# One trunk layer on one core: small products of the recurrence queued with the filler, three squares left unadded, the last gate pair in two halves of tokens

## The chip, the cores and the metric

The kernel runs on one core of one Trainium2 chip. The time is device microseconds of one execution; three executions of the kernel before gave 2769.55, 2764.9 and 2765.1 us, median 2765.1. A core has TensorE (PE; PEld is its loading of weights), VectorE (DVE), ScalarE (ACT), GpSimd (POOL) and SyncE (SP), which starts the transfers.

## The reference

1024 tokens, 2048 channels, one layer. An RMS norm over the channels of each token comes first; one combined projection makes the inputs of two branches. One is a recurrence over 16 heads of 64 (RWKV-7), the other attends to a selection of keys. Both are gated, joined and projected; then comes a second gate, which multiplies a projection of p, and a last RMS norm.

```python
def rms_norm(x, g, eps=NORM_EPS):
    xf = x.astype(jnp.float32)
    y = xf * lax.rsqrt(jnp.mean(xf * xf, axis=-1, keepdims=True) + eps)
...
# per head and step of the recurrence
        Sa = jnp.einsum('bhvk,bhk->bhv', S, a_t)
        S = (S * w_t[:, :, None, :] + Sa[..., None] * b_t[:, :, None, :]
             + v_t[..., None] * k_t[:, :, None, :])
        y = jnp.einsum('bhvk,bhk->bhv', S, r_t)
...
    bonus = jnp.sum(rh * kh * r_k.astype(f32), axis=-1, keepdims=True) * vh
...
# after both branches: h += W_out(concat); h += (p W_ple) * sigmoid(h W_pg); RMS norm
```

## The kernel before

Channels lie on the 128 partitions and tokens on the free axis, in two halves (hf) of TH = 512. A float32 projection product is made of three products of rounded parts (fp32r): wh·xh, wh·xl, wl·xh; wh is a copy by ScalarE, wl = w - wh a subtraction by GpSimd, in two pieces of 256 columns each. Small products in plain float32 take two passes of TensorE and stand in the trace as two matmuls.

No engine's order is written by hand. All operations are recorded, and a planner (`plan`, line 267) with costs and due times places each on its engine; each carries a level, and the lower one goes first. For TensorE it keeps three queues (line 304): ops under level LG = 3 are the work that is due; ops at LG and above are the filler, RUN = 3 of which may follow one another after a burst; ops with LEND = 0.5 wait for the end of a burst, or until they are WAIT = 3 us old, or until nothing else is there (lines 308 to 315). The transposes pk and pv (lines 720 and 729) and those of chunk_out (815) are LEND already.

Stages. (1) From 0 to some 1480 us: `load_xn` (484) loads 16 tiles of x for a half, splits them, and squares each (level LSQ) into xsum, by an add on VectorE; buffers zs (NZ = 3) hold the squares. `x_row` (470) takes the token sums by `token_sums` (477), a product of each 128 tokens of xsum with a column of ones; then a reciprocal root on GpSimd (rpow) and a spreading over the partitions by `bcast` (463), four transposes into a PSUM tile named cr. `zgroup` (550) is the combined projection. The recurrence goes over 8 units of two heads and their four quarters of 256 tokens, 32 sub-units, each of NCK = 4 chunks: `chunk_setup` (616) makes pA, pb2 (702) and, in `side_a` (709), pa, four products whose masked result is AA; `chunk_serial` (762) runs the chain pu, UV, pS, and ends each chunk with a product of AA and UV added to pY. These use the PSUM ring pi (3 buffers). (2) The key search and the attention, to some 2000 us; it starts with the products pg of hq and the scores pix of qs. (3) The end: `wout_ds` (1426) adds the output product for a half, with dh and dl from `split_mixed` (1380); `gate` (1448) makes, for each of 16 tiles, pl (6 products, tile pg), pz (48 products), tanh, the sum h2 and its square sq, which GpSimd adds to acc; `pss` are the token sums of acc and of the last square; `emit_out` (1475) makes rr and rb_, a copy of cr by ScalarE, scales each tile by it, eleven on VectorE and every third on ScalarE and GpSimd, and stores each tile (256 KB). Order as recorded: output product and gate of half 0, output product of half 1, output of half 0, gate of half 1, output of half 1. Rings at the end: 5 temporary tiles (tmp3), 5 raw weight tiles, 6 each of wh and wl, 2 buffers of pi. The level LEVAC = 1 of what leaves PSUM, and of emit_out(0), lies ahead of LG, at which the splits dh and dl and the products of the gate are recorded.

Of the kernel before, what the change touches and what calls it, by code (L numbers as in the profile page):

```python
# [20 lines left out]
D = 2048  # L21
# [364 lines left out]
def hybrid_kernel(ctx, tc, cst, msk, bkt, prm, xt, pt_, w_z, w_z80, w_lora, w_uq, w_iq, w_uk, w_uv, w_o, w_pg,  # L386
# [61 lines left out]
    sm = pool(ph1r, RP, name="sm", bufs=4, side="right")  # L448

    W_, PI = [NWR, NWH], [3]  # L450
    XH, XL, SB = [None] * 4, [None] * 4, [None] * 2

    def nhalf(dst):
        if len(dst.shape) == 2:
# [14 lines left out]

    def x_row(hf):  # L470
        sr = sm.tile([128, 4], F32, name="sr", bufs=1)
        nc.vector.tensor_scalar(sr, token_sums(SB[hf], 128), 1.0 / D, 1e-6, op0=OP.mult, op1=OP.add)
        rpow(sr, sr)
        SB[hf] = wp.tile([128, TH], F32, name="SB", tag="SB", bufs=1)
        nc.scalar.activation(SB[hf], bcast(sr), AF.Copy)

    def token_sums(t, n):

        pn = ps.tile([128, 4], F32, name="cn", tag="pi", bufs=PI[0])
        for i in range(4):  # L480
            nc.tensor.matmul(pn[:, i:i + 1], t[:n, i * 128:i * 128 + 128], one[:n], start=True, stop=True)
        return pn

    def load_xn(hf, g, piece=None):
        XH[g] = xn.tile([128, 4, TH], F32R, name=f"xh{g}", tag=f"xh{g}")
        XL[g] = xn.tile([128, 4, TH], F32R, name=f"xl{g}", tag=f"xl{g}")
        for k in range(4):
            if hf == 0:
                r = io.tile([128, TH], F32, name=("r", "k", "v", "gg")[k])
            else:  # L490
                r = wp.tile([128, TH], F32, name="xr", tag="wr", bufs=NWR)
            nc.sync.dma_start(r, xt[(g * 4 + k) * 128:(g * 4 + k + 1) * 128, hf * TH:hf * TH + TH])
            gc = col(P, PNG + g * 4 + k)
            nc.scalar.activation(XH[g][:, k, :], r, AF.Copy, scale=gc)
            nc.vector.scalar_tensor_tensor(XL[g][:, k, :], r, gc, XH[g][:, k, :], op0=OP.mult, op1=OP.subtract)
            with nc.level(LSQ):
                if g == k == 0:
                    SB[hf] = tp.tile([128, TH], F32, name="xsum", tag="zl", bufs=3)
                    nc.scalar.activation(SB[hf], r, AF.Square)
                else:  # L500
                    sq = tp.tile([128, TH], F32, name="zsq", tag="zs", bufs=NZ)
                    nc.scalar.activation(sq, r, AF.Square)
                    nc.vector.tensor_tensor(SB[hf], SB[hf], sq, op=OP.add)
            if piece and k in PIECES:
                piece()
# [110 lines left out]
    def chunk_setup(s_, u, t0, wa, lw_, tiles):  # L616
# [83 lines left out]
        for h in range(2):  # L700
            nc.scalar.activation(AB[hp(h), :, hp(h)], AR[hp(h), :, hp(h)], AF.Copy)
        pb2 = ps.tile([128, TQ], F32, name="pb2", tag="pi", bufs=3)
        nc.tensor.matmul(pb2, rkb, rk, start=True, stop=True)
        bonv = io.tile([128, TQ], F32, name="bonv", bufs=2)
        nc.vector.tensor_tensor(bonv, pb2, v, op=OP.mult)
        sl = lambda t: (lambda h, c: t[hp(h), c, :])
# [1 line left out]

        def side_a():
            pa = ps.tile([128, NCK, 128], F32, name="pa", tag="pi", bufs=3)  # L710
            for c in range(NCK):
                nc.tensor.matmul(pa[:, c, :], KB[:, c, :], BR[:, c, :], start=True, stop=True)
            nc.vector.tensor_tensor(AA, pa.rearrange("p c (h t) -> p c h t", h=2), c_("incl")[:, None, None, :].to_broadcast(
                [128, NCK, 2, 64]), op=OP.mult)

# [46 lines left out]
    def chunk_serial(u, last, after, AA, AB, Q, KBT, UV, BR, Wx, bonv):  # L762

        pY = ps.tile([128, NCK, 128], F32, name="pY", tag="py", bufs=1)
        if not after[1]:
            for h in HO:
                nc.scalar.activation(UV[hp(h), 0, hp(h)], S[u][hp(h)], AF.Copy)
        for c in range(NCK):  # L770
            pch = ps.tile([128, 3, 128], F32, name="pch", tag="pu", bufs=1)
            pr_, pu, pS = pch[:, 0], pch[:, 1], pch[:, 2]
            nc.tensor.matmul(pr_, AB[:, c, :], UV[:, c, :], start=True, stop=True)
            rh = sm.tile([128, 128], F32, name="rh", bufs=2)
            nc.vector.tensor_copy(rh, pr_)
            nc.tensor.matmul(pY[:, c, :], BR[:, c, :], UV[:, c, :], start=(c == 0), stop=False, skip_group_check=True)
            more = not (last and c == NCK - 1)
            if more:
                Sw = sm.tile([128, 64], F32, name="Sw", bufs=2)
                for h in HO:  # L780
                    nc.scalar.activation(Sw[hp(h)], UV[hp(h), c, hp(h)], AF.Copy, scale=Wx[hp(h), c, 64:65])
            nc.tensor.matmul(pu, Q[:, c, :], rh, start=True, stop=True)
            for h in HO:
                nc.scalar.activation(UV[hp(h), c, hp(h)], pu[hp(h), hp(h)], AF.Copy)
            if more:
                nc.tensor.matmul(pS, KBT[:, c, :], UV[:, c, :], start=True, stop=True)
                for h in HO:
                    if c < NCK - 1:
                        to = UV[hp(h), c + 1, hp(h)]
                    elif after[0] is not None:  # L790
                        to = after[0][hp(h), 0, hp(h)]
                    else:
                        to = S[u][hp(h)]
                    nc.vector.scalar_tensor_tensor(to, pS[hp(h), hp(h)], Wx[hp(h), c, 64:65], Sw[hp(h)],
                                                   op0=OP.mult, op1=OP.add)
            nc.tensor.matmul(pY[:, c, :], AA[:, c].rearrange("p h t -> p (h t)"), UV[:, c, :], start=False, stop=True,
                             skip_group_check=True)
        return pY

    def chunk_out(u, hf, q, y, bonv, gg):  # L800
# [23 lines left out]
    def sum_rows(zs, n):  # L824

        acc = None
        for z in zs:
# [2 lines left out]
            if acc is not None:  # L830
                nc.gpsimd.tensor_tensor(sq[:n], acc[:n], sq[:n], op=OP.add)
            acc = sq
        return token_sums(acc, n)

    def chan_rms(pn, width):
        a = sm.tile([128, 4], F32, name="ca", bufs=2)
# [224 lines left out]
    def pg_tile():  # L1061
        return g_pool[0].tile([128, 512], F32, name="pg", tag=g_pool[1])
# [382 lines left out]
            nc.vector.tensor_tensor(PL[:, k, :], r, PH[:, k, :], op=OP.subtract)  # L1445
        return PH, PL

    def gate(hf, HH, HL, PH, PL):
        H2 = []
        acc = tp.tile([128, TH], F32, name="acc", bufs=1)  # L1450
        for n in range(16):
            pl = pg_tile()
            gemm_part(pl, w_pl[n, 0], 128, 0, 2, 2, lambda k: PH[:, k, :], lambda k: PL[:, k, :])
            pz = gemm(lambda g: w_pg[n, g], 128, 16, lambda k: HH[k], lambda k: HL[k])
            with nc.level(LEVAC):
                tg = tmp3("tg3")
                nc.scalar.activation(tg, pz, AF.Tanh, scale=0.5)
                nc.vector.scalar_tensor_tensor(tg, tg, 1.0, pl, op0=OP.add, op1=OP.mult)
                h2 = mp.tile([128, TH], F32, name=f"h2{n}", tag=f"h2{n}")
                nc.vector.tensor_tensor(h2, HH[n], HL[n], op=OP.add)  # L1460
                nc.vector.scalar_tensor_tensor(h2, tg, 0.5, h2, op0=OP.mult, op1=OP.add)
                sq = acc if n == 0 else tmp3("sq3")
                nc.scalar.activation(sq, h2, AF.Square)
                if 0 < n < 15:
                    nc.gpsimd.tensor_tensor(acc, acc, sq, op=OP.add)
            H2.append(h2)
        pss = ps.tile([128, 4], F32, name="pss", tag="pss", bufs=1)
        with nc.level(LEVAC):
            for a in (acc, sq):
                for i in range(4):  # L1470
                    nc.tensor.matmul(pss[:, i:i + 1], a[:, i * 128:i * 128 + 128], one, start=(a is acc and i == 0),
                                     stop=(a is sq), skip_group_check=True)
        return H2, pss

    def emit_out(hf, H2, pss):
        ra = sm.tile([128, 4], F32, name="ra")
        nc.vector.tensor_scalar(ra, pss, 1.0 / D, 1e-6, op0=OP.mult, op1=OP.add)
        rr = sm.tile([128, 4], F32, name="rr")
        rpow(rr, ra)
        rb_ = tmp3("rb")  # L1480
        nc.scalar.activation(rb_, bcast(rr), AF.Copy)
        for n in range(16):
            if n % 3 == 2:
                nc.scalar.activation(H2[n], H2[n], AF.Copy, scale=col(P, PFG + n))
                nc.gpsimd.tensor_tensor(H2[n], H2[n], rb_, op=OP.mult)
            else:
                nc.vector.scalar_tensor_tensor(H2[n], H2[n], col(P, PFG + n), rb_, op0=OP.mult, op1=OP.mult)
            store(out[n * 128:n * 128 + 128, hf * TH:hf * TH + TH], H2[n])

    with nc.level(LG):  # L1490
        H0 = wout_ds(0)
        P0 = load_p(0)
        G0 = gate(0, *H0, *P0)
        P1 = load_p(1)
        H1 = wout_ds(1)
        with nc.level(LEVAC):
            emit_out(0, *G0)
        emit_out(1, *gate(1, *H1, *P1))
    nc.emit()
    ph3.close()  # L1500
    w2s.close()
# [39 lines left out]
```

## Time and profile before

| | |
|---|---|
| three executions, median | 2765.1 us (2764.9 to 2769.55) |
| the profiled execution | 2767.54 us |
| its span (first to last instruction) | 2765.7 us |
| mean granted clock of TensorE | 0.989 of full speed |
| TensorE busy | 2679.8 us, 97% of the span |
| VectorE, ScalarE, GpSimd busy | 1555.7, 1483.1, 1191.6 us |
| moved by DMA | 391.23 MB, 141 GB/s in the mean |

The profiled execution is one of the same program. Times of the trace count from the start of the span. In a row, `x8` is the number of instructions, and the time of a merged row runs from the start of the first to the end of the last; `out<-in` are the kernel's tile names; a wait is the idle time of the engine ahead of the instruction, with what released it. A matmul's duration includes its passing through the array, so one that follows another starts before the other's end.

### The profile page before, as it was taken

The page shows a single profiled execution, that of the slowest core. Times are in us where ns is not written, and L with a number is a line of the kernel's source. Part 1 is how long each engine was busy: PE and PEld are TensorE (multiplying, and loading weights), DVE is VectorE, ACT ScalarE, POOL GpSimd, SP SyncE. Part 2 cuts the span into 40 slices and gives each one's busy share as a digit, 9 for nine tenths or more (in the row PEclk, how much of TensorE's full clock was granted, in tenths as well). Part 3 has the DMA queues.
Part 4 walks back from the last instruction along what each step waited for, and adds up shares of the span by engine and source line. Part 5 has one row for each costly group of instructions (what it writes and reads, how often), then busy time and mean ns, then how long its engine had stood idle before and what let it go on. Part 6 is the DMA issues. An engine that isn't in the chain of part 4 may idle for free. (4 is left out here: it accounts for less than half of the span.)

```text
span 2765.7 us, 47714 instructions
## 1 busy us (share of the span) xinstructions
PE 2679.8 (97%) x16482; PEld 2150.6 (78%) x16482; DVE 1555.7 (56%) x3709; ACT 1483.1 (54%) x3265; POOL 1191.6 (43%) x1587
## 2 busy tenths in 40 slices
PE   7999999999999999999999999998999999999996
PEld 6777788877778777877787788786777778878885
DVE  5456676636674366666663678868767531135212
ACT  5445555535664355555554667786777533333331
POOL 7555556555411122222220543024433556657764
PEclk9999999999999999999999999999999999999998
DMA  7554444354454533334346557841222433355332
GB/s 235 156 183 124 134 141 142 119 170 136 138 191 157 168 120 122 124 124 125 124 132 192 161 202 241 269 153 52 75 81 85 153 105 98 96 165 176 99 97 93
DMA packets 229810, 391.23 MB, mean 141 GB/s; under 512 B 33552, under 2 KB 55104, under 8 KB 229568
## 3 DMA queue, kind: packets, MB, share of 16 engines
q1 hardware_dynamic: 229568, 388.18, 44.8%
q8 instruction: 130, 2.13, 0.3%
q14 instruction: 112, 0.92, 0.1%
HBM read 281.76 MB, written 101.08 MB: 138 GB/s over the span
## 5 line engine op out<-in xcount | busy, mean ns | idle before, releaser
L382 POOL TENSOR_TENSOR wl<-wr,wh 128x256 fp32r<-128x256 f32 (+1 forms) x840 | 664.6, 813 | 480.6 <-ACT wh L382 449.2
L382 ACT ACTIVATE wh<-wr 128x512 fp32r<-128x512 f32 (+1 forms) x624 | 383.5, 617 | 664.9 <-PE pz L382 534.5
L382 PE MATMUL pz<-xh,wh 128*128 128x512 f32 (+1 forms) x1504 | 611.1, 408 | 11.1 <-ACT wh L382 8.5
L382 PE MATMUL pz<-xl,wh 128*128 128x512 f32 (+1 forms) x1504 | 612.9, 409 | 0.0
L382 PE MATMUL pz<-xh,wl 128*128 128x512 f32 (+1 forms) x1504 | 607.8, 406 | 1.1 <-POOL wl L382 0.9
L382 PEld LDWEIGHTS pz<-xh,wh 128*128 128x128 f32 (+1 forms) x1504 | 286.0, 190 | 62.9 <-ACT wh L382 11.3
L382 PEld LDWEIGHTS pz<-xh,wl 128*128 128x128 f32 (+1 forms) x1504 | 285.2, 190 | 48.5 <-POOL wl L382 2.6
L382 PEld LDWEIGHTS pz<-xl,wh 128*128 128x128 f32 (+1 forms) x1504 | 285.7, 190 | 45.0
L382 PE MATMUL pz<-hl,wh 128*128 128x512 f32 x512 | 199.4, 390 | 0.1
L382 PE MATMUL pz<-hh,wh 128*128 128x512 f32 x512 | 199.3, 389 | 0.2 <-ACT wh L382 0.2
L382 PE MATMUL pz<-hh,wl 128*128 128x512 f32 x512 | 199.3, 389 | 0.0
L382 DVE SCALAR_TENSOR_TENSOR tg<-tg,pg 128x512 f32<-128x512 f32 x32 | 22.0, 687 | 308.7 <-ACT tg L382 297.4
L382 DVE CAST_PREDICATED QX<-MS,pq 128x512 f16<-128x512 uint8 x160 | 110.2, 689 | 134.6 <-PE pq L382 133.7
L382 ACT ACTIVATE Ztb<-pzt 64x256 f16<-64x256 f32 x320 | 120.5, 377 | 50.3 <-PE pzt L382 44.4
L382 POOL TENSOR_TENSOR mb<-mk,bt 128x256 f32<-128x256 f32 (+1 forms) x128 | 90.5, 711 | 117.8 <-DVE mx L382 101.6
L382 ACT ACTIVATE lgt<-lgt,nm 128x256 f32<-128x256 f32 (+7 forms) x128 | 98.7, 774 | 30.1 <-DVE nm L382 28.1
L382 PEld LDWEIGHTS pz<-hl,wh 128*128 128x128 f32 x512 | 96.1, 188 | 20.6 <-DVE hl L382 0.5
L382 PEld LDWEIGHTS pz<-hh,wh 128*128 128x128 f32 x512 | 96.1, 188 | 20.4 <-ACT wh L382 0.6
L382 PEld LDWEIGHTS pz<-hh,wl 128*128 128x128 f32 x512 | 96.1, 188 | 19.9
L382 ACT ACTIVATE scratch<-mk,th 128x1024 f16<-128x1024 f32 (+2 forms) x93 | 96.8, 1041 | 21.8 <-DVE xm L382 13.1
L382 ACT ACTIVATE PT<-ptt 128x512 f32<-128x512 f32 (+1 forms) x160 | 83.8, 551 | 43.1 <-PE ptt L382 41.7
L382 ACT ACTIVATE Sw<-UV,Wx 64x64 f32<-64x64 f32 x240 | 82.4, 343 | 44.5 <-DVE UV L382 40.3
(331 smaller groups left out, 5893.6 us busy)
## 6 DMA issues: line engine op xcount, KB each, us to landing
wr<-in_w_z_dram SPq DMA_DIRECT2D x368, 256.0 KB, 2.9
low<-wl SPq DMA_DIRECT2D x184, 256.0 KB, 3.2
wl<-low SPq DMA_DIRECT2D x184, 256.0 KB, 2.6
wr<-in_w_pg_dram SPq DMA_DIRECT2D x128, 256.0 KB, 2.6
wr<-in_w_o_dram SPq DMA_DIRECT2D x88, 256.0 KB, 2.9
h<-h SPq DMA_DIRECT2D x60, 256.0 KB, 3.5
h<-in_xt_dram SPq DMA_DIRECT2D x32, 256.0 KB, 3.4
out_dram<-h SPq DMA_DIRECT2D x32, 256.0 KB, 2.3
```

The costliest lines, as they stand in the source:

```text
L382: getattr(self.real[o.eng], o.name)(*o.args, **o.kw)
```

## The change

1. `pb2`, the four products pa of `side_a`, and the product of AA and UV that ends each chunk's pY are recorded at LEND.
2. In `load_xn`, the squares of the last three tiles (g == 3, k = 1 to 3) stay in their zs buffers; `token_sums` takes a list and adds the four operands in PSUM, 16 products instead of 4, in both halves of tokens.
3. `gate` of half 1 runs tiles 14 and 15 as two halves of 256 tokens each: both tiles for the first 256, then both for the second, with weights loaded, copied and split for each. Their squares are not added to acc. `emit_out` is called for each half of 256, with three operands of the token sums, and it now contains the pss products; VectorE scales from the PSUM tile pb (cr) itself, GpSimd's tiles still from the copy rb_. The h2 tiles become four group tiles of four, and a group is stored by one transfer: 1 MB for half 0, 512 KB for each half of half 1. For half 0, sums are acc and the square of tile 15 as before.

```diff
     def x_row(hf):
-        nc.vector.tensor_scalar(sr, token_sums(SB[hf], 128), 1.0 / D, 1e-6, op0=OP.mult, op1=OP.add)
+        nc.vector.tensor_scalar(sr, token_sums([SB[hf], *SQ[hf]], 128), 1.0 / D, 1e-6, op0=OP.mult, op1=OP.add)
...
-            nc.tensor.matmul(pn[:, i:i + 1], t[:n, i * 128:i * 128 + 128], one[:n], start=True, stop=True)
+            for t in ts:
+                nc.tensor.matmul(pn[:, i:i + 1], t[:n, i * 128:i * 128 + 128], one[:n], start=(t is ts[0]), stop=(t is ts[-1]))
...
             with nc.level(LSQ):
-                if g == k == 0:
+                if g == 3 and k > 0:
+                    sq = tp.tile([128, TH], F32, name="zsq", tag="zs", bufs=NZ)
+                    nc.scalar.activation(sq, r, AF.Square)
+                    SQ[hf].append(sq)
+                elif g == k == 0:
...
-        nc.tensor.matmul(pb2, rkb, rk, start=True, stop=True)
+        with nc.level(LEND):
+            nc.tensor.matmul(pb2, rkb, rk, start=True, stop=True)
...
-            for c in range(NCK):
-                nc.tensor.matmul(pa[:, c, :], KB[:, c, :], BR[:, c, :], start=True, stop=True)
+            with nc.level(LEND):
+                for c in range(NCK):
+                    nc.tensor.matmul(pa[:, c, :], KB[:, c, :], BR[:, c, :], start=True, stop=True)
...
-            nc.tensor.matmul(pY[:, c, :], AA[:, c].rearrange("p h t -> p (h t)"), UV[:, c, :], start=False, stop=True,
-                             skip_group_check=True)
+            with nc.level(LEND):
+                nc.tensor.matmul(pY[:, c, :], AA[:, c].rearrange("p h t -> p (h t)"), UV[:, c, :], start=False, stop=True,
+                                 skip_group_check=True)
...
+    def gate(hf, HH, HL, PH, PL, split=()):
+        H2[hf] = [mp.tile([128, 4, TH], F32, name=f"h2{hf}{g}", tag=f"h2{g}") for g in range(4)]
+        runs = [([n for n in range(16) if n not in split], (0, TH))]
+        runs += [(split, (t, t + TQ)) for t in range(0, TH, TQ)] if split else []
+        for ns, (t0, t1) in runs:
...
+                    if 0 < n < (14 if split else 15):
+                        nc.gpsimd.tensor_tensor(acc, acc, sq, op=OP.add)
+                    else:
+                        sqs.append(sq)
+            if ns is split:
+                with nc.level(LEVAC):
+                    emit_out(hf, [acc[:, t_], *sqs], t0, t1)
...
+    def emit_out(hf, sums, t0, t1):
+        pss = ps.tile([128, nb], F32, name="pss", tag="pss", bufs=1)
+        for j, a in enumerate(sums):
+            for i in range(nb):
+                nc.tensor.matmul(pss[:, i:i + 1], a[:, i * 128:i * 128 + 128], one, start=(i == j == 0),
+                                 stop=(j == len(sums) - 1), skip_group_check=True)
...
+                if n % 3 == 2:
+                    nc.scalar.activation(h2, h2, AF.Copy, scale=col(P, PFG + n))
+                    nc.gpsimd.tensor_tensor(h2, h2, rb_, op=OP.mult)
+                else:
+                    nc.vector.scalar_tensor_tensor(h2, h2, col(P, PFG + n), pb, op0=OP.mult, op1=OP.mult)
+            store(out[g * 512:g * 512 + 512, hf * TH + t0:hf * TH + t1].rearrange("(n p) t -> p n t", p=128),
+                  H2[hf][g][:, :, t0:t1])
...
-        emit_out(1, *gate(1, *H1, *P1))
+        gate(1, *H1, *P1, split=(14, 15))
```

## Rows read from the trace of the kernel before

**Rows 1.** The page's first part: busy us (share of the span), instructions, by engine.
```profile
PE 2679.8 (97%) x16482; PEld 2150.6 (78%) x16482; DVE 1555.7 (56%) x3709; ACT 1483.1 (54%) x3265; POOL 1191.6 (43%) x1587
```

**Rows 2.** Busy time by engine, 100 to 1480 us; then granted clock, DMA share, GB/s.
```profile
100.00:1480.00 1380.00, 1366.17 (x9531) 1086.93 (x9530) 825.43 (x1747) 744.11 (x1905) 509.60 (x723) 1.00 0.45 141
```

**Rows 3.** The chain that ended last, its end: start us, us, what.
```profile
2717.27 10.88 PE pz L382 x48
...
2728.15 1.36 PE pg L382 x6
...
2741.43 0.61 ACT tg L382
...
2746.16 0.17 DVE ra L382
...
2746.40 1.03 POOL rr L382
...
2747.47 1.13 PE cr L382 x4
```

**Rows 4.** Timeline of the end: start us, us, what [idle before, releaser].
```profile
2749.31 12.50 DVE L382 SCALAR_TENSOR_TENSOR h<-h,P,rb 128x512 f32<-128x512 f32 x11 [2.99 <-ACT rb L382]
2749.35 7.93 POOL L382 TENSOR_TENSOR h<-h,rb 128x512 f32<-128x512 f32 x5 [1.94 <-ACT rb L382]
2751.19 11.14 SPq L382 DMA_DIRECT2D out_dram<-h  x16
```

**Rows 5.** Timeline of a weight piece in the last gate tile: ScalarE, GpSimd.
```profile
2725.38 0.63 ACT L382 ACTIVATE wh<-wr 128x512 fp32r<-128x512 f32 x1 [2.09 <-PE pz L382]
...
2726.09 1.44 POOL L382 TENSOR_TENSOR wl<-wr,wh 128x256 fp32r<-128x256 f32 x2 [1.28 <-ACT wh L382]
```

**Rows 6.** Groups by form: busy us, mean ns of one, idle before and releasers.
```profile
L382 DVE SCALAR_TENSOR_TENSOR kkn<-k,P,pb 128x256 f32<-128x256 f32 x32 | 15.3, 478 | 11.5 <-PE pb L382 11.3
...
L382 DVE SCALAR_TENSOR_TENSOR zl<-zl,P,cr 128x512 f32<-128x512 f32 x10 | 7.0, 744 | 4.3 <-PE cr L382 4.2
...
L382 ACT ACTIVATE sq<-y 128x256 f32<-128x256 f32 x32 | 13.2, 413 | 8.0 <-DVE y L382 7.5
```

**Rows 7.** Timeline, TensorE, products of 256 columns in a row.
```profile
1844.90 0.40 PE L382 MATMUL pg<-lv,CH 128*128 128x256 f32 x2
1845.14 0.40 PE L382 MATMUL pg<-hv,CL 128*128 128x256 f32 x2
```

**Rows 8.** Timeline of the start, first half's token sums.
```profile
46.41 0.63 ACT L382 ACTIVATE zsq<-gg 128x512 f32<-128x512 f32 x1 [0.43 <-DVE xsum L382]
46.89 2.95 DVE L382 TENSOR_TENSOR xsum<-xsum,zsq 128x512 f32<-128x512 f32 x3 [0.52 <-DVE xsum L382]
...
49.90 1.87 PE L382 MATMUL cn<-one,xsum 128*128 128x1 f32 x8 [6.24 <-DVE xsum L382]
```

**Rows 9.** Timeline, TensorE, second half's token sums.
```profile
807.25 0.95 PE L382 MATMUL cn<-one,xsum 128*128 128x1 f32 x8
```

**Rows 10.** Timeline, TensorE, one sub-unit of the recurrence.
```profile
1195.13 0.59 PE L382 MATMUL pb<-rk,rkb 128*128 128x256 f32 x2
1195.56 1.05 PE L382 MATMUL pA<-ARb,KB 128*128 128x128 f32 x8
1196.45 1.06 PE L382 MATMUL pa<-BRb,KB 128*128 128x128 f32 x8
```

**Rows 11.** Timeline, from the first gate half to the second half's output product.
```profile
2454.90 1.05 PE L382 MATMUL pss<-one,sq 128*128 128x1 f32 x8 [1.88 <-ACT sq L382]
...
2464.18 1.96 DVE L382 TENSOR_TENSOR dl<-mraw,dh 128x512 fp32r<-128x512 f32 x2 [3.87 <-ACT dh L382]
...
2525.99 0.58 ACT L382 ACTIVATE rb<-cr 128x512 f32<-128x512 f32 x1
```

**Rows 12.** Waits of TensorE, 1480 to 1700 us: us in total, times, longest.
```profile
PE pix L382 <- DVE qs L382: 6.1, 1, 6.1
PE pg L382 <- ACT hq L382: 3.6, 1, 3.6
```

More of the change, by code (lines that the diff above doesn't have):

```diff
@@ L450, in hybrid_kernel @@
     W_, PI = [NWR, NWH], [3]
-    XH, XL, SB = [None] * 4, [None] * 4, [None] * 2
+    XH, XL, SB, SQ = [None] * 4, [None] * 4, [None] * 2, [[], []]
     def nhalf(dst):
@@ L475, in x_row, with token_sums @@
         nc.scalar.activation(SB[hf], bcast(sr), AF.Copy)
-    def token_sums(t, n):
+    def token_sums(ts, n):
         pn = ps.tile([128, 4], F32, name="cn", tag="pi", bufs=PI[0])
         for i in range(4):
-            nc.tensor.matmul(pn[:, i:i + 1], t[:n, i * 128:i * 128 + 128], one[:n], start=True, stop=True)
+            for t in ts:
+                nc.tensor.matmul(pn[:, i:i + 1], t[:n, i * 128:i * 128 + 128], one[:n], start=(t is ts[0]), stop=(t is ts[-1]))
         return pn
@@ L832, in sum_rows @@
             acc = sq
-        return token_sums(acc, n)
+        return token_sums([acc], n)
     def chan_rms(pn, width):
@@ L1446, in load_p @@
         return PH, PL
-    def gate(hf, HH, HL, PH, PL):
-        H2 = []
+    H2 = [None] * 2
+    def gate(hf, HH, HL, PH, PL, split=()):
+        H2[hf] = [mp.tile([128, 4, TH], F32, name=f"h2{hf}{g}", tag=f"h2{g}") for g in range(4)]
         acc = tp.tile([128, TH], F32, name="acc", bufs=1)
[L1451 to L1473, printed above, removed]
@@ L1475, in emit_out @@
-    def emit_out(hf, H2, pss):
-        ra = sm.tile([128, 4], F32, name="ra")
+        runs = [([n for n in range(16) if n not in split], (0, TH))]
+        runs += [(split, (t, t + TQ)) for t in range(0, TH, TQ)] if split else []
+        for ns, (t0, t1) in runs:
+            t_ = slice(t0, t1)
+            sqs = []
+            for n in ns:
+                pl = pg_tile()[:, :t1 - t0]
+                gemm_part(pl, w_pl[n, 0], 128, 0, 2, 2, lambda k: PH[:, k, t_], lambda k: PL[:, k, t_])
+                pz = pz_tile()[:, :t1 - t0]
+                for g in range(4):
+                    gemm_part(pz, w_pg[n, g], 128, 4 * g, 4, 16, lambda k: HH[k][:, t_], lambda k: HL[k][:, t_])
+                with nc.level(LEVAC):
+                    tg = tmp3("tg3")[:, :t1 - t0]
+                    nc.scalar.activation(tg, pz, AF.Tanh, scale=0.5)
+                    nc.vector.scalar_tensor_tensor(tg, tg, 1.0, pl, op0=OP.add, op1=OP.mult)
+                    h2 = H2[hf][n // 4][:, n % 4, t_]
+                    nc.vector.tensor_tensor(h2, HH[n][:, t_], HL[n][:, t_], op=OP.add)
+                    nc.vector.scalar_tensor_tensor(h2, tg, 0.5, h2, op0=OP.mult, op1=OP.add)
+                    sq = (acc if n == 0 else tmp3("sq3"))[:, :t1 - t0]
+                    nc.scalar.activation(sq, h2, AF.Square)
+                    if 0 < n < (14 if split else 15):
[3 more added lines that the diff above has]
+            if ns is split:
+                with nc.level(LEVAC):
+                    emit_out(hf, [acc[:, t_], *sqs], t0, t1)
@@ L1477, in emit_out @@
+        return acc, sqs[-1]
+    def emit_out(hf, sums, t0, t1):
+        nb = (t1 - t0) // 128
+        pss = ps.tile([128, nb], F32, name="pss", tag="pss", bufs=1)
[3 more added lines that the diff above has]
+                                 stop=(j == len(sums) - 1), skip_group_check=True)
+        ra = sm.tile([128, nb], F32, name="ra")
         nc.vector.tensor_scalar(ra, pss, 1.0 / D, 1e-6, op0=OP.mult, op1=OP.add)
-        rr = sm.tile([128, 4], F32, name="rr")
+        rr = sm.tile([128, nb], F32, name="rr")
@@ L1479, in emit_out @@
         rpow(rr, ra)
[L1480 to L1488, printed above, removed]
+        pb = ps.tile([128, TH], F32, name="cr", tag="pi", bufs=PI[0])[:, :t1 - t0]
@@ new lines, in emit_out @@
+        for i in range(nb):
+            nc.tensor.transpose(pb[:, i * 128:i * 128 + 128], rr[:, i:i + 1].to_broadcast([128, 128]), ident)
+        rb_ = tmp3("rb")[:, :t1 - t0]
+        nc.scalar.activation(rb_, pb, AF.Copy)
+        for g in range(4):
+            for n in range(4 * g, 4 * g + 4):
+                h2 = H2[hf][g][:, n % 4, t0:t1]
+                if n % 3 == 2:
[5 more added lines that the diff above has]
+                  H2[hf][g][:, :, t0:t1])
@@ L1492, in hybrid_kernel @@
         P0 = load_p(0)
-        G0 = gate(0, *H0, *P0)
+        sums = gate(0, *H0, *P0)
         P1 = load_p(1)
@@ L1496, in hybrid_kernel @@
         with nc.level(LEVAC):
-            emit_out(0, *G0)
-        emit_out(1, *gate(1, *H1, *P1))
+            emit_out(0, sums, 0, TH)
+        gate(1, *H1, *P1, split=(14, 15))
     nc.emit()
```

## The prediction

> **What bounds the kernel now.** I read the page's busy shares first: TensorE is busy 97% of the span, every other engine at most 56% [rows 1]. So only three things count: TensorE's own work, its few idle stretches, and what lies behind its last product. The recurrence is no idle stretch: from 100 to 1480 us TensorE is busy 1366.17 of 1380.00 us at full granted clock [rows 2]; its chain of small products is filled up with projection products. The chain of waits ends with the gate: one gate tile is 1.36 us of pg and 10.88 us of pz products, 12.24 us, and behind the last of them tanh (from 2741.43), squares, sums, reciprocal root and its spreading over the partitions follow one by one [rows 3]. The timeline of that end shows eleven scalings on VectorE, 12.50 us from 2749.31, beside five on GpSimd and 16 stores [rows 4]. The span ends at 2765.7, so 24.3 us stand behind the last product. The profiled execution took 2767.54 us, 1.84 more than its span and 2.4 more than the median of the runs; I sum differences and take them off the median.
>
> **Change 1: pb2, pa and the second pY product at the filling queue's place.** Nothing is added; 9 products in each of 32 sub-units change place. A pair of 256-column ones takes at most 0.59 us, eight of pa at most 1.06 us [rows 10], wherever they stand. TensorE runs without a gap there, so a product moved costs the same later: nothing, while filler is at hand. What it can bring is latency: pb2 and pa no longer stand ahead of the chain's next product (pb2, then pA, then pa is the order now [rows 10]), so the recurrence could end earlier; then filler must be found for the time after it. The waits to be filled stand at the start of the second stage: 3.6 us for hq and 6.1 us for qs [rows 12]. Against it: each of these ops now waits up to 3 us for a burst's end, and behind pa wait VectorE's mask (AA), behind that pY and the output of the unit; a buffer of the three in the ring pi is held as long. Bounds: -7, both waits (9.7) but for about a quarter that I leave to hq's and qs's own steps, and +5, the share of a gap where filler runs out (a third of the 13.8 us idle in rows 2). I take half the nearest wait, 3.6: **-1.8**.
>
> **Change 2: squares of three tiles unadded.** Removed: three adds of VectorE, 2.95 us from 46.89 to 49.84, which the start waits for; TensorE stood still 6.24 us before the sums [rows 8]. Added: 16 products for 4, and each is two passes: 8 passes took 1.87 us [rows 8], .234 a pass, at the lower level of the clock (1.2 GHz); in the second half 8 took 0.95 us, .119 a pass, at 2.4 GHz [rows 9]. Now the sums can begin when xsum of tile 12 is there, about 46.4 (its last-but-three add ends as the square starts at 46.41), or with the last square at 47.04. Then 32 passes x .234 = 7.5 us end at 53.9, against 51.77 now: +2.1. At the higher level 32 x .119 = 3.8 us end at 50.3: -1.5. The engine has been idle since 43.66 (49.90 - 6.24), and the sums of now ran at the lower level after such a gap, so I take **+2.1**, bounds -1.5 and +2.2. In the second half the sums stand in a full stream [rows 9]: 24 passes x .119 = 2.9 us more of TensorE; what idle time there is near it may take some of that, by rows 2 a mean of 13.8/32 = .4 per sub-unit: **+2.5**, bounds +1.8 and +2.9. The three adds saved there lie on VectorE, off the path.
>
> **Change 3: the last two gate tiles in two halves of 256 tokens.**
> *TensorE.* 108 products of 512 columns (2 x 54; 12.24 us per tile [rows 3], 24.5) become 216 of 256. A pair of 256-column products stands .24 us from the next (1844.90 to 1845.14 [rows 7]), .12 each: 25.9 us, +1.4. The first half's sums and its transposes now run in the stream: 12 passes x .119 + .3 = +1.7.
> The Trainium skill ("TensorE: Matmul & The Clock Gate", section "Back-to-back issue gap") gives N/2.4 + 2.5 ns for a lone product, so by an estimate from it 109 ns, 23.6 us and -0.9 instead of +1.4; the rows say .12, and I keep them.
> *GpSimd.* It now splits the two tiles' weights twice: four pieces of 1.44 us [rows 5] and one of half the size per tile and half, 20 pieces, 25.9 us. It is about four pieces ahead (its ring has six buffers), which leaves 20.2; the first half's output adds rr, 1.0 [rows 3], and five products of half width, 7.93/5/2 = .8 each [rows 4]: 25.2 us for pieces that the products need after about 24. I take **+1.4** of waiting, bounds 0 and 3. ACT's copies (0.63 each [rows 5]) have room. So TensorE ends 1.4 + 1.7 + 1.4 = 4.5 later (3.1 to 6.1).
> *Behind TensorE.* Only 256 tokens are left. Tanh, two DVE steps and the square by rows of 256 columns: about .41, .48, .48, .41 [rows 6] and .16 of handing over = 1.9; the sums, four passes for the last operand (the other two wait in front) x .131 (1.05/8 [rows 11]) = .5; ra .24, rr 1.07 and .07 of handing over as now [rows 3]; four transposes took 1.13 [rows 3], two about .6; no copy rb for VectorE; eleven scalings from PSUM x .478 [rows 6] = 5.3 against 12.50 [rows 4]. Then the store: now the span ends 3.9 us after the last scaling (2749.31 + 12.50); the last store grows from 256 to 512 KB, and 4 MB take 14.5 us now (16 stores from 2751.19 [rows 4]), so +.9: 4.8. Sum 1.9 + .5 + 1.38 + .6 + 5.3 + 4.8 = 14.5 for 24.3: -9.8. Net **-5.3**, bounds -9 (no GpSimd wait, .12 kept, the store as now) and -2 (full GpSimd wait, a store that waits behind another).
> On the scalings from PSUM the Trainium skill speaks against the change ("VectorE: DVE Perf Modes", section "Rules for kernel authors": take single speed on matmul output, or copy it to SBUF first where many ops follow). The trace differs: from PSUM 512 columns take 744 ns [rows 6], from the copied rb 12.50/11 = 1136 ns beside GpSimd [rows 4]. With the second figure's half, .57, the tail is 1.0 longer.
> *The first half's output* now has 11 scalings of .744 [rows 6] that read cr itself, and are free as soon as cr is there, about 2458.5 (2454.90 + 1.05 [rows 11], then 1.38 and cr's 1.13 as at the end). Before, they waited for rb (2525.99 [rows 11]). I cost this at 0 with its cover named: VectorE has only the dl splits to do there, and TensorE has pieces up to k = 7 until about 2466 (2464.18 + 1.96 [rows 11]). If that cover fails, it is rival 3.
>
> **Sum**: -5.3 + 2.1 + 2.5 - 1.8 = -2.5; 2765.1 - 2.5 = **2762.6**.
>
> **Rivals.**
> 1. *The recurrence hands over its lead* (faster): units end early and the whole of the two waits is covered [rows 12]: -2.5 + 1.8 - 7 = -7.7, **2757.4**. For: pb2 and pa stand on the order of every unit [rows 10]. Against: filler is spent once, and the search for the keys that follows is not waited for by TensorE alone.
> 2. *Sums at the higher level and GpSimd in step* (faster): the first sums come after a gap that is 3.5 us shorter (46.4 for 49.90) and take 3.8 us for 7.5, 3.6 us less, and GpSimd's 1.4 is not waited for: -2.5 - 3.6 - 1.4 = -7.5, **2757.6**. Against: the clock was at the lower level right after the same idle stretch [rows 8].
> 3. *Scalings ahead of the splits* (slower): with the output of the first half free at 2458.5, VectorE does 11 x .744 = 8.2 us of them ahead of the four dl splits left, which have the lower rank; dl of k = 4 and on started at 2464.18 and were just in time for TensorE [rows 11]. If the fifth split comes 8.2 us later, the next raw tile's copy (.63 [rows 5]) and split (1.96/2 [rows 11]) come behind it: about 10 us of TensorE waiting, -2.5 + 10 = +7.5, **2772.6**. It decides from the point where more than about five scalings stand ahead of the fifth split (3.87 us idle there [rows 11], 5 x .744 = 3.7). Against: the planner puts an op by its ready time, and stores or reading of cr may come late.
> 4. *The tail is as long as before* (the change doesn't do what it says): the last half's stores, 2 MB at 4 MB in 14.5 us = 7.3 us, queue behind the first half's and set the end whenever the scalings are done; the tail brings 0 instead of -5.3, +2.8 in all, **2767.9**.
>
> **How the numbers follow.** Forecast .48 (2758.5 to 2766.5), rival 1 .17, rival 2 .18, rival 3 .13, rival 4 .04. The measurement can tell about 0.2%, 5.5 us, from no change. Rivals 1 and 2 are beyond it (.35), the forecast and rival 4 within (.52), rival 3 beyond on the other side (.13). For 8 in 10 the range reaches to rivals 1 and 2 with some of their own width, and to 2771 on the other side, where it leaves most of rival 3 out: 2753 to 2771.
>
> **What would show it.** The first sums at 46.4 or 47.0 with 7.5 us (step right) or under 4 us (rival 2). The recurrence's last unit and hq's wait at 1519: shorter by 1 to 4 us (right), gone with qs's (rival 1), longer (wrong). In the last gate pair products .12 us apart and a GpSimd wait of about 1.4 us. A tail of 14 to 15 us behind the last product; 20 or more is rival 4. At 2458 to 2470 the order on VectorE: scalings ahead of dl with TensorE idle for several us is rival 3. The prediction falls if TensorE's sum of work in the second half's sums and the gate grows by clearly more than 2.9 + 1.4 + 1.7 = 6.0 us, or if the second stage shifts by more than 7 us either way.

## The result and the profile after

The changed kernel takes 2900.02 us (median, 2895.07 to 2902.79) beside 2765.0 for the kernel before: ratio 1.0485, 95% interval 1.0469 to 1.0500, 4.9% slower. The prediction was 2762.6, range 2753 to 2771. The profiled execution has a span of 2896.4 us, against 2765.7.

TensorE's line of the page's first part, of the changed kernel, beside rows 1:

```profile
PE 2729.1 (94%) x16646; PEld 2192.7 (76%) x16646; DVE 1547.9 (53%) x3721; ACT 1492.5 (52%) x3285; POOL 1175.1 (41%) x1610
```

TensorE is busy 49.3 us longer and 94% of the time instead of 97% (14.6 of the 49.3 belong to the second and third part of the change: without the first it is busy 2694.4 us). So there are two losses: the engine stands still longer, and its work takes longer. The busy time by stretches of the changed kernel (columns as in rows 2) says where:

```profile
100.00:1480.00 1380.00, 1335.80 (x8861) 1066.11 (x8861) 748.77 (x1567) 688.70 (x1727) 480.43 (x690) 0.97 0.45 140
400.00:1000.00 600.00, 570.26 (x3667) 455.04 (x3666) 315.99 (x662) 294.75 (x731) 226.53 (x319) 0.95 0.44 136
1910.00:2100.00 190.00, 117.41 (x750) 84.35 (x751) 143.14 (x594) 138.18 (x285) 54.57 (x77) 0.75 0.14 37
```

Up to 1480 us TensorE has done 8861 matmuls where it had done 9531 [rows 2], at a granted clock of 0.97; and between 1910 and 2100 it stands still for 73 of 190 us, at 0.75. The first is the recurrence. Its last product is the second pY product, here the tile view of it in the changed kernel (duration minimum/median/maximum in ns, then first and last start in us):

```profile
L382 PE MATMUL pY<-UV,AA x256: 270/275/562, 131.6 to 1648.8; 128*128 128x128 f32 x128
```

and in the kernel before:

```profile
L382 PE MATMUL pY<-UV,AA x256: 270/275/421, 123.4 to 1486.8; 128*128 128x128 f32 x128
```

The recurrence ends 162 us later. The second is what follows. The search for the keys on VectorE can begin only then, and the attention waits for it. VectorE's counting operations of that search ran from 1694.2 to 1850.7 before; in the changed kernel:

```profile
L382 DVE TENSOR_SCALAR_CACHE_REDUCE scratch<-mk,th x102: 595/740/1271, 1842.3 to 2002.8; 128x640 f16<-128x640 f32 x32, 128x512 f16<-128x512 f32 x32, 128x384 f16<-128x384 f32 x32, 128x1024 f16<-128x1024 f32 x2
```

Before, TensorE had output products (pz of mh) to do until 1824.2, beside that search. Now it has done a good part of them earlier, as filler of the longer recurrence; they end at 1878.6, and the search goes on to 2003. The waits of TensorE between 1900 and 2110 (us in total, times, longest) show what it is left with, above all:

```profile
PE plg L382 <- DVE mx L382: 52.1, 9, 23.4
```

plg is the score of the attention. The profile names mx as its releaser, but VectorE is busy with the search at the time (above), so the 23.4 us at 1943 to 1967 are waits for the search.

### The profile page after: what moved, and what is told of

Same layout as the page of the kernel before. It is cut to its first block, busy times and chain, and to the rows that moved or that the text cites. A ratio compares the mean times of both kernels' runs of the same rounds, so it can differ in the third digit from the quotient of the medians.

```text
span 2896.4 us, 48078 instructions
## 1 busy us (share of the span) xinstructions
PE 2729.1 (94%) x16646; PEld 2192.7 (76%) x16646; DVE 1547.9 (53%) x3721; ACT 1492.5 (52%) x3285; POOL 1175.1 (41%) x1610
## 5 line engine op out<-in xcount | busy, mean ns | idle before, releaser
L382 POOL TENSOR_TENSOR wl<-wr,wh 128x256 fp32r<-128x256 f32 (+1 forms) x858 | 657.2, 788 | 461.8 <-ACT wh L382 430.5
L382 PE MATMUL pz<-xh,wh 128*128 128x512 f32 (+1 forms) x1504 | 613.2, 409 | 14.5 <-ACT wh L382 9.2
L382 PE MATMUL pz<-hh,wh 128*128 128x512 f32 (+1 forms) x544 | 205.1, 377 | 0.2 <-ACT wh L382 0.2
L382 PE MATMUL pz<-hl,wh 128*128 128x512 f32 (+1 forms) x544 | 205.2, 377 | 0.1
L382 PE MATMUL pz<-hh,wl 128*128 128x512 f32 (+1 forms) x544 | 205.0, 377 | 0.0
L382 DVE SCALAR_TENSOR_TENSOR tg<-tg,pg 128x512 f32<-128x512 f32 (+1 forms) x34 | 22.3, 657 | 305.8 <-ACT tg L382 305.7
L382 PE MATMUL plg<-kh,qs 128*128 128x512 f32 (+3 forms) x192 | 76.0, 404 | 53.7 <-DVE mx L382 52.9
L382 PEld LDWEIGHTS pz<-hh,wh 128*128 128x128 f32 x544 | 102.3, 188 | 19.4 <-ACT wh L382 0.6
L382 PEld LDWEIGHTS pz<-hl,wh 128*128 128x128 f32 x544 | 102.3, 188 | 19.3 <-DVE hl L382 0.5
L382 PEld LDWEIGHTS pz<-hh,wl 128*128 128x128 f32 x544 | 102.3, 188 | 18.6
L382 ACT ACTIVATE UV<-pch 64x64 f32<-64x64 f32 x256 | 55.3, 216 | 107.3 <-PE pch L382 104.1
```

The lines of the kernel that those rows point to most:

```text
L382: getattr(self.real[o.eng], o.name)(*o.args, **o.kw)
```

## Why the recurrence got longer

The instruction order of TensorE and the trace tell the same. Ten sub-units of the second half took 359.9 us before (the pb2 at 1014.84 to the one at 1374.73) and 440.8 us in the changed kernel (1083.57 to 1524.34), 8.1 us more each. In them stand 964 filler products before and 1288 now: 32 more for each sub-unit, some 7.4 us at .23. So in this stretch nearly all of the lengthening is filler, put in where the chain's products used to stand. And the stretches of filler have a length of their own: 15 of them are of exactly 14 products, against 2 before. Here is one, TensorE's timeline of the changed kernel:

```profile
1059.99 0.27 PE L382 MATMUL pv<-C,v 128*128 128x128 f32 x1
1060.02 0.47 PE L382 MATMUL pz<-xh,wl 128*128 128x512 f32 x1
...
1063.30 0.27 PE L382 MATMUL pv<-C,v 128*128 128x128 f32 x1
...
1065.01 0.39 PE L382 MATMUL pch<-UV,AB 128*128 128x128 f32 x2
```

The same step in the kernel before:

```profile
1062.71 0.27 PE L382 MATMUL pv<-C,v 128*128 128x128 f32 x1
1063.96 0.27 PE L382 MATMUL pv<-C,v 128*128 128x128 f32 x1
```

The two transposes pv stand 3.31 us apart instead of 1.25. UV is made of pv, and the chain of the next sub-unit (pch of UV and AB) cannot start without it. 3.3 us is the planner's limit WAIT = 3 for an op of the end queue. pv and pk were in that queue already. The planner takes one op from it at the end of a burst of due work (when run is 0), and no second one while filler is running; then only the limit helps. Before, 8 such ops came in a sub-unit (4 pk, 2 pv, 2 pc) and there were 19 stretches of filler to begin with one. Now 17 come to 21 stretches: enough over the whole sub-unit, but not in the few us in which pk and pv are wanted. The queue serves the op that has been ready longest; pb2 and pa take the first turns, pk comes later, and pv last. Once the chain waits for pv, no burst comes whose end could serve it, and TensorE does filler until the limit.

The trace bears this out over all 32 sub-units (medians of the start times on TensorE, counted from the last pA product): the first pk comes at 10.4 us (4.1 before), the last pk at 14.9 (9.4), the two pv stand 3.30 us apart (1.60), and the chain's first pch comes at 23.5 (16.1). In 21 of the 32 the two pv are over 2.8 us apart, in none before. So it is pv that runs into the limit; the pk still find ends of bursts, only later (19 of their 96 distances are over 2.8 us, 3 before).

That the moved ops take the turns of pk and pv is **theory 1**. **Theory 2**: the other two parts (squares, halved pair, scalings ahead of the splits) carry a good share. **Theory 3**: each op from the end queue lets a run of three fillers begin (.7 us), which the due work then sits out, so it is the number of ops in the queue that costs, whichever they are.

## The experiments

Times are compared with runs of the kernel before on the same chip. The counts of filler in the expectations are those of TensorE's instruction order; they hold 640 products pzt of the recurrence, which are no filler. The trace has 4328 filler products (pz) ahead of the last pY before and 4723 in the changed kernel; the differences that the expectations use are not touched by this.

**Undo the first part** (pb2, pa, pY due again):

```diff
-        with nc.level(LEND):
-            nc.tensor.matmul(pb2, rkb, rk, start=True, stop=True)
+        nc.tensor.matmul(pb2, rkb, rk, start=True, stop=True)
...
```

The products pa and the second pY product likewise.

> The changed kernel without its first part: pb2, pa and the second pY product are due work again; the unadded squares and the halved gate pair stay. Theory 1 (the whole loss comes from the end queue): the recurrence ends near 1487 us again (its order holds 4968 filler products ahead of the last pY, as before; 5363 in the changed kernel), and the time is that of my sum without its first term, -5.3 + 2.1 + 2.5 = -0.7, so 2764 us, between 2757 and 2772. Theory 2 (the halved gate pair, the sums or the output of the first half in front of the splits cost the greater part): over 2800 us.

Measured: 2768.81 us, ratio 1.0003 (0.9992 to 1.0013); the last pY starts at 1494.0. The whole loss is the first part's; theory 2 falls. (The last pY is 7.2 us later than before, not near 1487, but the time is not.)

**The first part alone**, on the kernel before (the same lines, the other way).

> The kernel before with the first part of the change alone (pb2, pa, second pY product wait in the end queue). Theory 1: the whole loss, 2900 us (2885 to 2915), and the recurrence's last pY near 1649 us. Theory 2: under 2830 us.

Measured: 2903.68 us, ratio 1.0487 (1.0469 to 1.0505); the last pY starts at 1644. As theory 1 said.

**Only pk back among the due work**, everything else as changed:

```diff
             pk = ps.tile([128, NCK, 128], F32, name="pk", tag="pi", bufs=3)
-            with nc.level(LEND):
-              for c in range(NCK):
+            for c in range(NCK):
                 nc.tensor.transpose(pk[:, c, :], KB[:, c, :], ident)
```

> The changed kernel with the four transposes pk, which stood in the end queue before already and feed the chain, made due work; pb2, pa and pY stay in the end queue. Theory 1 (the ops that joined the queue take the ends of bursts away from pk, and pk is then left to the limit of 3 us): the recurrence ends near 1490 us (4978 filler products ahead of its last pY), time 2755 to 2775 us. Theory 3 (each of the 9 ops per sub-unit that joined opens a run of three fillers, .7 us, which the due work sits out, so 9 x .7 = 6 us per sub-unit): all nine are still there, so over 2860 us.

Measured: 2775.03 us, ratio 1.0023 (1.0013 to 1.0034), at the upper end of what theory 1 said. An op that the change didn't touch, taken out of the queue, gives back 95% of the loss, with pb2, pa and pY still delayed. Theory 3 falls (all nine ops that joined are there, and the time is 6.4 us over before, not over 90), and so does the thought that the delay of pa or pY itself costs. TensorE's timeline of this kernel:

```profile
1036.94 0.60 PE L382 MATMUL pk<-C,KB 128*128 128x128 f32 x4
...
1039.32 0.27 PE L382 MATMUL pv<-C,v 128*128 128x128 f32 x1
1040.56 0.27 PE L382 MATMUL pv<-C,v 128*128 128x128 f32 x1
```

The four pk stand together, and pv finds ends of bursts again, 1.24 us apart. Ten sub-units take 359.9 us, as before, with 960 fillers. The run doesn't say that it must be pk: it leaves 13 ops in the queue for 17, and the last pk itself comes hardly earlier than in the kernel before (9.2 us behind the last pA product, 9.4 before). What it gives back are turns, and pv takes them. No run takes four other ops out, or pv alone.

**The condition that the queue is served only right after a burst, dropped:**

```diff
-                    pick = last if last and run == 0 and fill else fill
+                    pick = last if last else fill
```

> The changed kernel with one condition of the planner dropped: an end op may be taken whenever nothing due is ready, not only as the first thing after a burst. Theory 1: pk is no longer left to the 3 us, 5041 filler products ahead of the last pY, 73 more than before x .227 us = 17 us later recurrence; time 2765 to 2800 us. Theory 3: every end op still opens its run of three fillers, so over 2860 us.

Measured: 2785.45 us, ratio 1.0056 (1.0039 to 1.0072). All 17 ops are still in the queue, and 88% of the loss is gone: it was the standing in the queue, not the number of ops by itself. The two pv stand 1.27 us apart in the median, in none of the 32 sub-units over 2.8.

**The limit at 1 us:**

```diff
-RUN, RUNX, LEND, WAIT = 3, 0, 0.5, 3
+RUN, RUNX, LEND, WAIT = 3, 0, 0.5, 1
```

> The changed kernel with the limit after which an end op is taken anyway at 1 us instead of 3. Theory 1: pk and pv are left standing for 1 us each instead of 3, 5149 filler products ahead of the recurrence's end, 181 more than before: x .24 (as in the run with the dropped condition) = 43 us, or x .34 (as in the changed kernel) = 62 us, so 2808 to 2830 us. Theory 3 (runs of three fillers): more ops run into the limit and each opens a run, so no faster than the changed kernel, 2900 us or more.

Measured: 2792.19 us, ratio 1.0096 (1.0080 to 1.0111), 27 us over before, below the 2808 to 2830 that I had put down. Its TensorE timeline, of the same step as above in another sub-unit:

```profile
1096.19 0.27 PE L382 MATMUL pv<-C,v 128*128 128x128 f32 x1
...
1097.46 0.33 PE L382 MATMUL pv<-C,v 128*128 128x128 f32 x1
```

1.3 us apart now, for 3.3 in the changed kernel; in ten sub-units the runs of 14 fillers are gone, and there are 33 of 5, for 12 in the changed kernel and 24 before. The wait follows the constant. Ten sub-units take 380.9 us with 1074 fillers, 21 us more than before, although the chain's first pch comes as early as before (the table below). So at least a part of this run's 27 us has another cause, which is not taken apart; that each op taken lets in some filler (theory 3, at a smaller price) is not excluded for it. What I had wrong is the price of a filler product placed too early: 181 more cost 27 us (.15 each), 73 more in the run above 15.5 us (.21), 395 in the changed kernel 134 us (.34). It isn't constant.

**One kind of op alone in the queue**, on the kernel before: pa, then the second pY product (two of the three hunks of the first part, each by itself; pb2 alone was not run).

> The kernel before with pa alone in the end queue (four more products per sub-unit there). Theory 1 (what counts is how much filler is placed ahead of the recurrence's end because pk is left waiting): 4989 filler products against 4968, 21 x .24 = 5 us, ratio 1.000 to 1.004. Theory 3 (each op in the end queue opens a run of three fillers that the due work sits out): 32 x 4 x .7 = 90 us at the most, and at least 40 us, ratio over 1.014.

> The kernel before with the second pY product alone in the end queue. Theory 1: 5040 filler products ahead of the recurrence's end, 72 more, x .24 = 17 us, ratio 1.004 to 1.009. Theory 3: as for pa, over 1.014.

Measured: pa alone 2767.92 us, ratio 1.0007 (0.9997 to 1.0017); pY alone 2770.56 us, 1.0020 (1.0011 to 1.0029), 5.5 us where I had put down 17 and a ratio of at least 1.004. Twelve ops in the queue still find enough ends of bursts.

**pa and pY together** (the changed kernel with pb2 due):

> The changed kernel with pb2 due again; pa and the second pY product stay in the end queue. Each of the two alone cost little (ratio 1.0007 and 1.0020). Theory 1: together they take the burst ends away from pk as in the changed kernel, 5410 filler products ahead of the recurrence's end against 5363 there, so 2890 us or more. Rival (the costs of the parts add up and the greater part is pb2's): 2768 + 2 + 6 = 2776 us, under 2800.

Measured: 2864.38 us, ratio 1.0359 (1.0343 to 1.0375). The two cost 2 and 5.5 us alone and 99 us together. So the costs don't add; there is a point between 12 and 16 ops for a sub-unit at which pk and pv are left without turns. My expectation was 2890 or more, from 5410 fillers against 5363; the time is 36 us below that of all three, so that count ranks kernels only roughly. What pb2 adds to the 99 us is not taken apart here.

The runs side by side (first the ops in the queue for each sub-unit; then medians over the 32 sub-units: start of the last pk and of the chain's first pch, in us from the last pA product, and the distance of the two pv; then in how many sub-units that is over 2.8 us):

| kernel | ops | last pk | pv to pv | over 2.8 | first pch | last pY starts | ratio |
|---|---|---|---|---|---|---|---|
| before | 8 | 9.4 | 1.60 | 0 | 16.1 | 1486.8 | |
| first part undone | 8 | 9.4 | 1.60 | 0 | 16.1 | 1494.0 | 1.0003 |
| pa alone | 12 | 10.3 | 1.83 | 5 | 16.7 | 1498.1 | 1.0007 |
| pY alone | 12 | 10.4 | 1.69 | 6 | 16.6 | 1502.8 | 1.0020 |
| pk due | 13 | 9.2 | 1.25 | 0 | 16.1 | 1501.0 | 1.0023 |
| pa and pY | 16 | 14.3 | 3.30 | 24 | 22.0 | 1618.2 | 1.0359 |
| first part alone | 17 | 14.9 | 3.30 | 21 | 23.5 | 1643.8 | 1.0487 |
| changed | 17 | 14.9 | 3.30 | 21 | 23.5 | 1648.8 | 1.0485 |
| condition dropped | 17 | 12.1 | 1.27 | 0 | 17.2 | 1514.8 | 1.0056 |
| limit 1 us | 17 | 9.9 | 1.26 | 0 | 16.2 | 1547.3 | 1.0096 |

The kernels that are slower by over 3% are those in which pv waits for the limit of 3 us in most sub-units.

**The third part alone**, the halved gate pair (the changed kernel without the first two parts):

> The kernel before with the third part of the change alone: gate tiles 14 and 15 of the second half in two halves of 256 tokens, scalings from PSUM, grouped stores. From the trace of the kernel without the first part: TensorE's last product 4.5 us later and the tail 8.4 us shorter, so 3.9 us faster than before, ratio 0.9986 (0.997 to 1.000). Rival (the part brings nothing, since the kernel without the first part was as fast as before, and the sums cost nothing either): ratio 1.000 or above.

Measured: 2760.97 us, ratio 0.9985 (0.9975 to 0.9995): 4.1 us faster than the kernel before.

**The second part alone**, the unadded squares on the kernel before:

> The kernel before with the unadded squares alone (16 products of token sums for 4 in each half, three adds fewer). From my steps +2.1 at the start and +2.5 in the second half: 4.6 us slower, ratio 1.0017 (1.0005 to 1.003). Rival (the sums are hidden or the start gains): 1.000 or below.

Measured: 2771.08 us, ratio 1.0018 (1.0009 to 1.0027), 5.0 us slower. It costs what the halved pair gains, which is why the changed kernel without its first part is as fast as before.

## The prediction, step by step

**Change 1: wrong, and it is nearly the whole error** (the other two together: -0.7 forecast, +0.8 measured). I put -1.8 with bounds -7 and +5; alone it costs 135 us. The step that failed is "a product moved costs the same later: nothing, while filler is at hand". It asked what the moved products cost, and who waits for them (AA, pY, a buffer of pi); it did not ask who stands in the queue that they were moved into. pk and pv stood there, are of the chain, and had it to themselves but for pc. I had named the transposes as members of that queue in the description of the kernel, and the 3 us limit as a cost of the moved ops, but never put the two together. The second half of the same error: "TensorE runs without a gap there", from rows 2, was read as safety. It is the opposite. Where filler covers every gap, a longer chain isn't seen as idle time at once; it uses up filler, and the gap appears where that filler is missing. Here that is in two places: later, in the attention (52.1 us of waits for plg), and in the recurrence itself, above all between 400 and 1000 us, where TensorE is busy 570.26 us (593.74 before) and waits for the chain itself (for UV 7.5 us, Ztb 6.1, rh 3.4).

One sign of change 1 came out although its reason failed: the waits for hq and qs are 1.3 and 1.4 us in the changed kernel, for 3.6 and 6.1 [rows 12]. The recurrence ended later, not earlier, so this is not the gain that I meant.

The account, changed kernel against the one without the first part (spans 2896.4 and 2766.9): TensorE's idle time (span less busy time) is 167.3 us against 72.5, +94.8; its busy time is 2729.1 against 2694.4 for the same 16646 matmuls, +34.7. Of the idle time, 39.7 us more stand between 100 us and the last pY (52.3 against 12.6), and 54.0 behind it (99.6 against 45.6). The busy time is longer because more of the work ran at the lower of the clock's two levels (granted 0.5, 1.2 GHz): 121.0 us of it against 52.1 by the trace's records of the granted clock, and half of the difference of 68.9, 34.5, is what the higher level would have saved. Most of it lies in the stretches in which TensorE also stands still (mean granted clock 0.75 between 1910 and 2100 and 0.93 between 400 and 700, where the other kernel had 1.00 in both).

**Change 2: right in the sum, one of its two terms too small.** +2.1 at the start: pz resumes at 57.88 in the kernel without the first part, 2.25 us later than the 55.63 of before (59.11 with the sums alone, 3.5 later). Within it one number was off. TensorE's timeline there:

```profile
47.59 0.38 PE L382 MATMUL cn<-one,xsum 128*128 128x1 f32 x2 [2.38 <-DVE xsum L382]
47.84 1.05 PE L382 MATMUL cn<-one,zsq 128*128 128x1 f32 x6
48.75 0.56 PE L382 MATMUL cn<-one,xsum 128*128 128x1 f32 x2
49.18 1.42 PE L382 MATMUL cn<-one,zsq 128*128 128x1 f32 x6
```

The sums start at 47.59, a little after 46.4 to 47.0, and the first eight passes still run at the higher level of the clock (1.16 us to 48.75, .15 each), the rest mostly at the lower (.23): 6.4 us instead of 7.5. Rival 2's higher level was there for a quarter of the passes.

The second half's +2.5 was too small in the traces: between the sub-units at 769 and at 945 us the lag behind the kernel before grows from 3.3 to 7.5 us without the first part, and from 3.0 to 9.1 with the sums alone, so by 4.2 and 6.1. I had counted passes at the higher level only; between 770 and 950 us these two kernels have 10.2 and 13.7 us at the lower level, the kernel before 3.4. That the whole is +5.0 by the times and +4.6 by the forecast is in part luck: with the sums alone the lag is 9.2 us at the last pY, and how it shrinks behind the recurrence is not taken apart.

**Change 3: right in sign and mechanism.** -5.3 forecast, -4.1 measured. The end of the kernel with the third part alone, timeline:

```profile
2743.82 1.05 PE L382 MATMUL pss<-one,sq 128*128 128x1 f32 x8 [2.69 <-ACT sq L382]
...
2745.90 0.69 PE L382 MATMUL cr<-C,rr 128*128 128x128 f32 x2 [1.03 <-POOL rr L382]
...
2747.10 4.40 DVE L382 SCALAR_TENSOR_TENSOR h<-h,P,cr 128x256 f32<-128x256 f32 x11 [2.03 <-ACT rb L382]
```

The tail behind TensorE's last pz is 15.97 us (span 2757.1, last pz done at 2741.13) where I put 14.5 and it was 24.35 (last pz done at 2741.39). The eleven scalings take 4.40 us, less than the 5.3 I had: one lasts .476, as I took from rows 6, but the next starts .40 after it; but squares to sums are 2.7 us (1.9 in my sum), as the two tiles' steps queue on VectorE and ScalarE; two operands' sums stand behind it, eight passes, not four (1.05 for .5); VectorE's scalings start behind rb all the same (2747.10, after ScalarE's copy, .5 later than cr), and the stores take 5.6 us after the last scaling (4.8). Ahead of the end, the last gate pair itself cost 2.9 us (from the start of pz of tile 13 to the last pz: 39.41 us in the kernel without the first part, 36.52 before), as 1.4 + 1.7 = 3.1 said; the 1.4 us of waiting for GpSimd didn't come (the only wait there is 0.2 us for a square). So the tail was 1.5 us longer than I put it and TensorE's end 1.6 us earlier: that the sum is near is in part two errors that cancel.

**The rivals.** Rival 3 did not happen. VectorE's timeline after the first gate half, kernel without the first part:

```profile
2469.74 0.81 DVE L382 TENSOR_TENSOR dl<-mraw,dh 128x512 fp32r<-128x512 f32 x1 [5.21 <-ACT dh L382]
...
2538.53 2.07 DVE L382 SCALAR_TENSOR_TENSOR h<-h,P,cr 128x512 f32<-128x512 f32 x3 [0.96 <-ACT rb L382]
```

The scalings stand 70 us behind the splits, after rb's copy, as in rows 11. They read cr, which is there from 2462.4 on, but the planner put them behind rb's copy all the same; why is not shown by these rows. Rival 1 falls: with the first part alone the recurrence's last pY starts 157 us later, not earlier. Rival 4 falls: the tail is 8.4 us shorter. Of rival 2, the GpSimd wait stayed away as it said, the higher clock came for a quarter of the sums. No rival of mine was the one that came, though I had its parts.

## What to carry to other kernels

Before you move an operation into a queue that is served by turns, list who is in it already and count the turns, in the stretch where they are wanted: the cost falls on the member that the critical chain waits for (here pv), and most of it comes at once when the turns run out (2 and 5.5 us alone, 99 us together). In a schedule that fills gaps with independent work, a busy engine is no sign of slack: watch when the chain ends and how much filler stands ahead of that, since a longer chain is paid for wherever the filler is missing, mostly later. A run length that repeats (14 fillers, 3.3 us) points to a constant of the scheduler, and changing that constant is a cheap test.

## What the runs showed of the hardware that was not expected

VectorE's scaling of 128x512 became steady when it read the PSUM tile cr in place of the copy rb. The tile views (ns, minimum/median/maximum), of the kernel before and of the one without the first part:

```profile
L382 DVE SCALAR_TENSOR_TENSOR h<-h,P,rb x22: 737/1201/1853, 2526.6 to 2761.1; 128x512 f32<-128x512 f32 x22
...
L382 DVE SCALAR_TENSOR_TENSOR h<-h,P,cr x33: 472/474/749, 2538.5 to 2760.9; 128x256 f32<-128x256 f32 x22, 128x512 f32<-128x512 f32 x11
```

GpSimd does its own scalings beside both. In a row, one of 512 columns from cr starts .69 us after the other (2.07/3), with rb 1.14 [rows 4], and one of 256 columns from cr .40 (4.40/11). What makes those with rb so uneven was not taken apart. For a matmul's output the Trainium skill ("VectorE: DVE Perf Modes", section "Rules for kernel authors") offers single speed from PSUM, or a copy to SBUF first where many operations follow; in these rows the copy is the slower way for this operation. A 256-column product of the gate keeps .12 us from the next, as rows 7 had it.
